# A two-layer transformer trunk on one core: the mirroring of the tokens' mean squares in two steps, and new tables for the order of the work

## The chip, the cores and the metric

The kernel runs on one core of a Trainium2 chip. Its engines each work through a queue of their own, in order: TensorE (PE in the profile; PEld is its loading of weights), VectorE (DVE), ScalarE (ACT), GpSimd (POOL) and SyncE (SP), which here only issues transfers; GpSimd issues some too. The metric is the device time of one execution in microseconds, of which the runs shown give the median.

## The reference

256 tokens of width 2048 pass through two layers, all in float32. What matters here:

```
h = h + attention(rms_norm(h) @ w_in) @ w_out          # layer 1: causal, with forget gates
h = h + relu(rms_norm(h) @ w1)**2 @ w2                 # MLP, inner width 8192
k, v = split(rms_norm(h) @ kv_w)                       # shared keys and values, computed once
q = rms_norm(h) @ w_q
h = h + chunked_attention(q, k, v, rel_bias) @ w_out   # layer 2
h = h + relu(rms_norm(h) @ w1)**2 @ w2
```

Every matrix has 2048 rows (w2 has 8192), so nearly all the work is products of 256 tokens with weights that are read once from memory.

## The kernel before

**Exact products from split weights.** Each weight tile of 128 x 1024 (a *unit*) is taken apart: ScalarE makes a rounded high half (L310, `hi`), VectorE the rest of it (L319, `lo`). TensorE multiplies the activations, split in the same way, three times: high with high (L628), low with high (L630), high with low (L632). So TensorE needs the high half at the start of a unit and the low half at its last third. The function `fetch` hands out the next unit and first writes out as many low and high halves ahead as a table says.

**The pairs.** The two MLPs run in four chunks of the inner width each. One chunk has four *pairs* of column blocks: w10 and w11 (first matrix), w20 and w21 (second matrix). Behind the first MLP stand two further pairs for the query of layer 2, q0 and q1. Within a pair a part of the product is done by seven products in place of eight (Winograd's form of Strassen's method), on weight blocks 11, 12, 21, 22 and their sums. These are the forms f0 to f6, whose weights are 11, T3 = 12 + 22, T2 = T3 + 11, T1 = 11 + 12, 21, T4 = T2 + 21, and 22. A form has two halves of six products each. The rest of a pair are eight *plain* units of twelve products, four called a and four called b. The even pairs (w10, w20, q0) gather in the PSUM tiles `s` and `po`, the odd ones (w11, w21, q1) in `acc`.

The sums of blocks come from several queues. `bring` (L337) has SP fetch block 11 or 12 into a tile of its own, which is free when the pair before is done with it. GpSimd adds blocks from memory onto them for T3 and T1 (L350, a transfer that accumulates). VectorE makes T2 (L357, `make`) and T4 (L348). T4 reads block 21 from the buffer in which it was loaded as a unit; that buffer, one of three of `raw` (loaded at L295 by SP), is free only when both additions for T4 are done.

Between forms, partial sums pass from one PSUM tile to another: behind f0 and f1 by ScalarE (L668, L671), behind f2 by VectorE's subtraction L673, behind f3 by L675. f3 adds onto the tile that L673 reads, so its first product waits for L673.

**The order is written out by tables.**
- `ORDER` gives each pair's forms (f0 to f6), own plain units (a, b) and, as r, plain units that the pair ahead has left over. An r takes nothing where nothing is left. What a pair doesn't name it leaves to the next.
- `LOOK` gives for f0 to f6 and for plain units how many units beyond the present one are made ready before its products are written out; `MORE` allows that many high halves more.
- `BEHIND` hangs `make`, `add` and `bring` behind the low half of a form: (form, half): (how many low halves later, whether for this pair (1) or the next (0), what, ...).
- `HIDDEN`, `LONG`, `SHORT`, `AGAIN`, `QUERY` give, in units (a form counts as one), how long after the end of a column block each step of its further work comes. `HIDDEN` is for the hidden layer's four column blocks: four moves that finish the transposition of a block by transfers (L490; SP and GpSimd issue two each per move), and then relu, square and split (L990 to L1001). `LONG` and `SHORT` are for the stages that make the next layer's input: squares of rows, transpose, four moves, then scaling by the gains (L451), and split (L454, L455). `SHORT` serves the stage ahead of each MLP.
- `OPENING` does for the first pair of an MLP what `BEHIND` does for the others.

These steps are put into the list `fill`; `run_fill` takes one entry after each plain unit and each form.

**The mirroring.** Layer 2's keys and values are computed with the tokens in mirrored order, so the tokens' mean squares (`ms`, 128 x 2) must be mirrored over the partitions as well. `flip` (L611 to L620) does it with a product: VectorE copies the identity matrix with its columns reversed (`flipper`, L614), TensorE multiplies `ms` by it (L615), VectorE copies the result (L618) and scales it (L568), GpSimd takes a power of it (L563). It is one entry of `fill`, `QUERY[6]` = 3 entries behind the end of q0's second column block, which lies in the middle of q1. From there the order of before is f3, b, a, b, with the mirroring behind that b, then f6, a, a, b, b and the first panel of the keys. That panel writes the tiles `acc` that q1 used, so it waits for the norms of the query (L731, `qn`) that still read them.

Of the kernel before, what the change touches and what calls it, by code (L numbers as in the profile page):

```python
# [15 lines left out]
P = 128  # L16
# [27 lines left out]
)  # L44
SHORT = (
# [4 lines left out]
)  # L50
REL = 384
QUERY = (0, 1, 13, 10, 5, 9, 3)
AGAIN = (0, 0, 1, 3, 4, 4, 7, 5)
ATT = ((8, 14, 18, 18, 10), (8, 8, 12, 12, 9), (8, 13, 18, 18, 10), (8, 8, 12, 12, 8))
BIAS = ((3, 6, 7), (3, 6, 4))
LOOK = {
# [6 lines left out]
}  # L63
MORE = {
# [6 lines left out]
}  # L71
ORDER = {
# [9 lines left out]
}  # L82
BEHIND = {
    "w10": {(0, 0): [(0, 1, "make", 0), (7, 1, "add", "T1", 0)], (0, 1): [(2, 1, "add", "T1", 1), (0, 1, "make", 1)], (1, 1): [(1, 0, "bring", "12", 0), (0, 0, "bring", "12", 1)], (3, 1): [(6, 0, "bring", "11", 0), (6, 0, "bring", "11", 1)], (4, 0): [(1, 1, "add", "T4", 0)], (4, 1): [(0, 1, "add", "T4", 1), (9, 0, "add", "T3", 1)], (6, 0): [(0, 0, "add", "T3", 0)]},
    "w11": {(0, 0): [(0, 1, "make", 0), (7, 1, "add", "T1", 0)], (0, 1): [(2, 1, "add", "T1", 1), (0, 1, "make", 1)], (1, 1): [(1, 0, "bring", "12", 0), (1, 0, "bring", "12", 1)], (3, 1): [(5, 0, "bring", "11", 0)], (4, 0): [(0, 1, "add", "T4", 0)], (4, 1): [(0, 1, "add", "T4", 1), (9, 0, "add", "T3", 1)], (6, 0): [(1, 0, "add", "T3", 0)], (2, 1): [(7, 0, "bring", "11", 1)]},
# [30 lines left out]
def trunk(ctx: ExitStack, tc: tile.TileContext, t):  # L116
# [454 lines left out]
    class RowStats:  # L571
# [27 lines left out]
        def spread(self):  # L599
# [9 lines left out]
            yield  # L609

        def flip(self):  # L611
            pm = ps_o.tile([P, 512], F32, name="pt", tag="po")
            flipper = wk.tile([P, P], F32, name="flipper", tag="wk")
            V.tensor_copy(flipper, ident[:, ::-1])  # L614
            TE.matmul(pm[:, :NB], flipper, self.ms, start=True, stop=True)  # L615
# [463 lines left out]
    def query(g):  # L1079
        box = {}  # L1080

        def f(b, ps):
# [124 lines left out]
```

## Time and profile before

| | |
|---|---|
| median of 3 runs | 2105.89 us (2103.67 to 2107.0) |
| the profiled execution's own time | 2103.45 us |
| its span | 2101.7 us, granted clock 0.999 |
| instructions | 26998 |

A row of the timeline has the start in us from the span's beginning, the duration in us, the engine, the line of the code, the operation, what it writes and reads, how many of the same kind follow one another (xN), and in brackets how long the engine idled before it and what ended that. SPq rows are issues of transfers by SP, whose data land later. In a row of waits stand engine, tile and line that waited, then what released it, then the total in us, how many times, and the longest. A row of the chain of waits has start, duration and what the time went to. A row of a stretch has its ends, its length, the busy time and count of PE, PEld, DVE, ACT and POOL, the granted clock, the busy share of the 16 transfer engines and GB/s.

### The profile page before, as it was taken

The numbers are of one execution on the slowest core, as the hardware profiler recorded it, in microseconds if no ns is written. First come the engines' busy times: TensorE is split into PE (matmuls) and PEld (weight loads), VectorE is DVE, ScalarE is ACT, GpSimd is POOL, SyncE is SP. The second block draws the span as 40 slices with busy tenths as digits, with TensorE's granted clock in tenths as the row PEclk, the third lists the DMA queues.
The fourth block names the chain that finished last, engine by engine and source line by source line (L and its number), as shares of the span: only waits on it lengthen the run. The fifth ranks groups of instructions, "written<-read, shape, count | busy, mean of one in ns | idle before, by whom it ended". The sixth has DMA issues, their size and how long they took to land. (4 is left out here: it accounts for less than half of the span.)

```text
span 2101.7 us, 26998 instructions
## 1 busy us (share of the span) xinstructions
PE 2069.0 (98%) x9114; PEld 1696.5 (81%) x9114; DVE 1723.8 (82%) x2003; ACT 1290.3 (61%) x1567; POOL 354.8 (17%) x552
## 2 busy tenths in 40 slices
PE   9999999999999999999999999999999999999999
PEld 7888888787887887887777888887878878878877
DVE  6777676898888889888999576768988998898896
ACT  6544545776667567567777444456765765675674
POOL 1001001231032022022224000022310310220220
PEclk9999999999999999999999999999999999999999
DMA  8777778899898898899886777688997988988884
GB/s 304 242 254 225 238 245 277 259 254 274 258 285 244 250 297 246 264 267 282 251 252 202 260 238 239 226 276 254 265 282 251 271 258 262 286 255 258 267 270 167
DMA packets 160635, 538.89 MB, mean 256 GB/s; under 512 B 42848, under 2 KB 68080, under 8 KB 125680
## 3 DMA queue, kind: packets, MB, share of 16 engines
q1 hardware_dynamic: 129136, 453.78, 60.8%
q0 software_dynamic: 31360, 83.39, 21.4%
q8 instruction: 71, 1.16, 0.2%
q14 instruction: 68, 0.56, 0.1%
HBM read 497.20 MB, written 15.75 MB: 244 GB/s over the span
## 5 line engine op out<-in xcount | busy, mean ns | idle before, releaser
L319 DVE TENSOR_TENSOR lo<-raw,hi 128x1024 fp32r<-128x1024 f32 (+1 forms) x634 | 753.4, 1213 | 149.7 <-ACT hi L310 137.4
L310 ACT ACTIVATE hi<-raw 128x1024 fp32r<-128x1024 f32 (+1 forms) x634 | 651.0, 1052 | 330.0 <-PE acc L630 129.6
L628 PE MATMUL acc<-hi,act 128*128 128x512 f32 x1644 | 456.1, 394 | 5.6 <-ACT hi L310 2.0
L632 PE MATMUL acc<-lo,act 128*128 128x512 f32 x1644 | 449.0, 390 | 1.7 <-DVE lo L319 1.7
L630 PE MATMUL acc<-hi,act 128*128 128x512 f32 x1644 | 448.8, 389 | 0.0
L628 PEld LDWEIGHTS acc<-hi,act 128*128 128x128 f32 x1644 | 306.8, 188 | 71.1 <-ACT hi L310 3.6
L632 PEld LDWEIGHTS acc<-lo,act 128*128 128x128 f32 x1644 | 307.9, 188 | 68.4 <-DVE lo L319 4.3
L630 PEld LDWEIGHTS acc<-hi,act 128*128 128x128 f32 x1644 | 308.5, 188 | 65.2 <-DVE act L421 0.5
L319 DVE TENSOR_TENSOR lo<-w,hi 128x1024 fp32r<-128x1024 f32 x204 | 243.8, 1214 | 18.6 <-ACT hi L310 18.4
L310 ACT ACTIVATE hi<-w 128x1024 fp32r<-128x1024 f32 x204 | 211.3, 1053 | 73.3 <-PE po L630 29.8
L490 POOL DMA_DIRECT2D q<-z x336 | 170.3, 517 | 259.1 <-DVE z L475 95.0
L310 ACT ACTIVATE hi<-wT 128x1024 fp32r<-128x1024 f32 x136 | 140.8, 1054 | 77.4 <-DVE wT L348 48.5
L319 DVE TENSOR_TENSOR lo<-wT,hi 128x1024 fp32r<-128x1024 f32 x136 | 160.3, 1216 | 4.8 <-ACT hi L310 3.7
L628 PE MATMUL s<-hi,act 128*128 128x512 f32 x476 | 136.7, 391 | 4.5 <-ACT hi L310 2.8
L632 PE MATMUL s<-lo,act 128*128 128x512 f32 x476 | 137.0, 392 | 0.6 <-DVE lo L319 0.5
L630 PE MATMUL s<-hi,act 128*128 128x512 f32 x476 | 136.0, 390 | 0.0
L628 PEld LDWEIGHTS s<-hi,act 128*128 128x128 f32 x476 | 89.0, 188 | 25.2 <-ACT hi L310 4.1
L632 PEld LDWEIGHTS s<-lo,act 128*128 128x128 f32 x476 | 88.5, 188 | 22.8 <-DVE lo L319 4.8
L630 PEld LDWEIGHTS s<-hi,act 128*128 128x128 f32 x476 | 88.7, 188 | 19.7 <-DVE act L1001 1.4
L727 POOL TENSOR_TENSOR rn<-vv,mhalf 128x4 f32<-128x4 f32 x32 | 44.4, 1401 | 336.3 <-DVE vv L726 336.2
L350 POOL DMA_DIRECT2D w<-in_f1a x32 | 28.6, 967 | 320.4 <-ACT hi L310 191.2
L357 DVE TENSOR_TENSOR wT<-w,w 128x1024 f32<-128x1024 f32 x68 | 82.7, 1217 | 0.0
(183 smaller groups left out, 2333.4 us busy)
## 6 DMA issues: line engine op xcount, KB each, us to landing
raw<-in_w_in SPq DMA_DIRECT2D x94, 512.0 KB, 5.3
raw<-in_s1a SPq DMA_DIRECT2D x32, 1024.0 KB, 6.8
raw<-in_s2a SPq DMA_DIRECT2D x32, 1024.0 KB, 6.7
raw<-in_w_kv SPq DMA_DIRECT2D x64, 512.0 KB, 5.6
raw<-in_s1b SPq DMA_DIRECT2D x32, 1024.0 KB, 6.7
raw<-in_s2b SPq DMA_DIRECT2D x32, 1024.0 KB, 5.7
raw<-in_w_oa SPq DMA_DIRECT2D x32, 512.0 KB, 5.6
w<-in_f1a SPq DMA_DIRECT2D x16, 1024.0 KB, 6.7
```

What stands on the lines that cost most here:

```text
L310: S.activation(hi[:, c], raw[:, c], AF.Copy)
L319: V.tensor_tensor(lo[:, c], raw[:, c], hi[:, c].bitcast(F32), op=ALU.subtract)
L350: G.dma_start(d, p.big[block][:, half(s)], accum_op=ALU.add)
L357: V.tensor_tensor(p.t["T2"][:, half(s)], p.t["T3"][:, half(s)], p.t["11"][:, half(s)], op=ALU.add)
L490: (SY, G)[j % 2].dma_start(d[32 * j : 32 * j + 32, i], z[32 * i : 32 * i + 32, j * n : (j + 1) * n])
L628: TE.matmul(ps, xh, cut(hi, j), start=first, stop=False, **kw)
L630: TE.matmul(ps, xl, cut(hi, j), start=False, stop=False, **kw)
L632: TE.matmul(ps, xh, cut(lo, j), start=False, stop=last, **kw)
L727: G.tensor_tensor(rn, vv, mhalf, op=ALU.pow)
```

## The change

`flip` gets a second `yield`: the reversed copy is one step, product and all that follows are another, two entries of `fill` later. It begins at `QUERY[6]` = 4 rather than 3. The PSUM tile is taken in the second step.

All the tables are replaced. Taking from `ORDER` what an r really takes, most orders stay as they were. What differs: in w21 one plain unit fewer stands ahead of f6 and one fewer behind f5, so that the next w10 has seven units of its forerunner to place rather than five; in w11 one a moves ahead of f3; in the last chunk's w21 f1 comes ahead of f0; in q1 the tail is f3, b, b, a, a, f6, a, b, b. In w20, T4's first addition comes one low half behind f4's first one rather than two. In w10, w21 and q1 it comes behind the same low half rather than one later. In `HIDDEN` the moves of the second, third and fourth column block come up to two entries sooner.

```diff
 HIDDEN = (
     (3, 3, 3, 5, 8, 9, 9, 10, 11, 12),
-    (0, 2, 3, 3, 5, 7, 7, 7, 9, 9),
-    (1, 1, 3, 3, 5, 5, 8, 9),
-    (1, 3, 4, 4, 7, 8, 9, 9),
+    (1, 2, 2, 2, 5, 7, 7, 7, 9, 9),
+    (0, 1, 1, 2, 5, 5, 7, 9),
+    (0, 1, 4, 4, 7, 8, 9, 9),
 )
 LONG = (
-    (0, 0, 1, 2, 2, 2, 7, 8, 8, 8),
-    (1, 1, 2, 3, 4, 4, 7, 8, 8, 11),
-    (4, 0, 0, 0, 1, 5, 7, 7),
-    (2, 0, 2, 3, 3, 3, 8, 8),
+    (2, 0, 0, 2, 2, 2, 8, 8, 8, 8),
+    (2, 1, 2, 3, 4, 4, 8, 8, 8, 10),
+    (4, 0, 0, 1, 3, 4, 7, 7),
+    (1, 0, 1, 3, 3, 3, 7, 8),
 )
 SHORT = (
-    (7, 0, 0, 0, 1, 1, 4, 5, 6, 6),
-    (9, 0, 1, 1, 5, 7, 8, 12, 13, 14),
-    (1, 0, 1, 1, 2, 4, 5, 8),
-    (8, 0, 1, 2, 2, 3, 4, 4),
+    (8, 0, 0, 0, 0, 1, 4, 4, 8, 8),
+    (7, 0, 1, 1, 5, 7, 8, 12, 13, 14),
+    (2, 0, 1, 4, 4, 4, 6, 8),
+    (7, 0, 1, 2, 2, 3, 5, 5),
 )
-QUERY = (0, 1, 13, 10, 5, 9, 3)
-AGAIN = (0, 0, 1, 3, 4, 4, 7, 5)
+QUERY = (0, 1, 14, 11, 7, 8, 4)
+AGAIN = (0, 0, 2, 2, 4, 4, 6, 5)
-BIAS = ((3, 6, 7), (3, 6, 4))
+BIAS = ((3, 6, 7), (8, 5, 3))
 LOOK = {
-    "w10": (2, 1, 2, 2, 3, 2, 2, 2),
-    "w11": (2, 3, 2, 2, 3, 2, 2, 2),
-    "w20": (2, 1, 2, 2, 1, 2, 2, 2),
-    "w21": (2, 2, 2, 1, 2, 1, 2, 2),
-    "q0": (2, 2, 2, 2, 1, 2, 1, 2),
-    "q1": (2, 2, 2, 2, 3, 2, 2, 2),
+    "w10": (2, 1, 2, 2, 2, 2, 3, 2),
+    "w11": (2, 3, 2, 2, 2, 2, 2, 2),
+    "w20": (2, 1, 2, 2, 1, 1, 3, 2),
+    "w21": (2, 2, 2, 1, 1, 1, 1, 2),
+    "q0": (2, 2, 1, 2, 1, 2, 2, 2),
+    "q1": (2, 3, 2, 2, 2, 2, 2, 2),
 }
...
 ORDER = {
-    "w10": "f0 r r r f1 f2 r f4 f5 f3 a r r a f6 r b a a b",
-    "w11": "f0 f1 r f2 r r r f4 f3 a a a r r f5 a f6 b b",
-    "w20": "r f0 r f1 f2 f4 r f3 f5 a r r a b f6 r",
-    "w21": "f0 f1 f2 r r f3 r f4 r r r r a f6 f5 r a b r",
+    "w10": "f0 r r r f1 f2 r f4 r f5 f3 a r a f6 b r a a b",
+    "w11": "f0 f1 r f2 r r f4 r a f3 a a f5 r a f6 r b b",
+    "w20": "r f0 r f1 f2 f4 r r f3 f5 a r a r r b f6 r",
+    "w21": "f0 f1 f2 r r f3 r f4 r r r r f6 f5 r r a",
...
-    "w21+": "f0 f1 r r f2 r r r r f4 f5 r f3 a r a f6 r a a r r b r b",
+    "w21+": "f1 f0 r r f2 r r r f4 r f5 f3 r r a a r f6 a a r b r r b",
...
-    "q1": "f0 f1 f2 r r a f4 r f5 r f3 b r b r a b f6",
+    "q1": "f0 f1 f2 r r a f4 r f5 r f3 b r b a a f6 r a",
 }
 BEHIND = {
...
-    "w20": {(0, 0): [(7, 1, "add", "T1", 0), (0, 1, "make", 0)], (0, 1): [(0, 1, "make", 1)], (1, 1): [(0, 0, "bring", "12", 0), (1, 0, "bring", "12", 1), (3, 1, "add", "T1", 1)], (3, 1): [(5, 0, "bring", "11", 0), (2, 0, "bring", "11", 1)], (4, 0): [(2, 1, "add", "T4", 0)], (4, 1): [(0, 1, "add", "T4", 1), (8, 0, "add", "T3", 1)], (6, 0): [(0, 0, "add", "T3", 0)]},
+    "w20": {(0, 0): [(7, 1, "add", "T1", 0), (0, 1, "make", 0)], (0, 1): [(0, 1, "make", 1)], (1, 1): [(0, 0, "bring", "12", 0), (3, 1, "add", "T1", 1), (1, 0, "bring", "12", 1)], (3, 1): [(5, 0, "bring", "11", 0), (1, 0, "bring", "11", 1)], (4, 0): [(1, 1, "add", "T4", 0)], (4, 1): [(0, 1, "add", "T4", 1), (7, 0, "add", "T3", 1)], (6, 0): [(0, 0, "add", "T3", 0)]},
...
 }
 OPENING = (
-    (18, "bring", "12", 0),
+    (16, "bring", "12", 0),
     (19, "bring", "12", 1),
-    (9, "add", "T3", 0),
-    (5, "add", "T3", 1),
+    (4, "add", "T3", 0),
+    (6, "add", "T3", 1),
     (4, "bring", "11", 0),
     (14, "bring", "11", 1),
 )
         def flip(self):
-            pm = ps_o.tile([P, 512], F32, name="pt", tag="po")
             flipper = wk.tile([P, P], F32, name="flipper", tag="wk")
             V.tensor_copy(flipper, ident[:, ::-1])
+            yield
+            pm = ps_o.tile([P, 512], F32, name="pt", tag="po")
             TE.matmul(pm[:, :NB], flipper, self.ms, start=True, stop=True)
...
             self.flipped = f
+            yield
...
-                    add_fill([[]] * QUERY[6] + [[st2.flip]])
+                    step = steps(st2.flip)
+                    add_fill([[]] * QUERY[6] + [[step], [], [step]])
```

More of the change, by code (lines that the diff above doesn't have):

```diff
@@ new lines @@
+    "w10": {(0, 0): [(0, 1, "make", 0), (8, 1, "add", "T1", 0)], (0, 1): [(2, 1, "add", "T1", 1), (1, 1, "make", 1)], (1, 1): [(1, 0, "bring", "12", 0), (0, 0, "bring", "12", 1)], (3, 1): [(7, 0, "bring", "11", 0), (4, 0, "bring", "11", 1)], (4, 0): [(0, 1, "add", "T4", 0)], (4, 1): [(0, 1, "add", "T4", 1), (9, 0, "add", "T3", 1)], (6, 0): [(1, 0, "add", "T3", 0)]},
+    "w11": {(0, 0): [(0, 1, "make", 0), (6, 1, "add", "T1", 0)], (0, 1): [(2, 1, "add", "T1", 1), (0, 1, "make", 1)], (1, 1): [(3, 0, "bring", "12", 0)], (3, 1): [(4, 0, "bring", "11", 0)], (4, 0): [(0, 1, "add", "T4", 0)], (4, 1): [(0, 1, "add", "T4", 1), (8, 0, "add", "T3", 1)], (6, 0): [(1, 0, "add", "T3", 0)], (2, 1): [(7, 0, "bring", "11", 1), (2, 0, "bring", "12", 1)]},
@@ new lines @@
+    "w20": {(0, 0): [(7, 1, "add", "T1", 0), (0, 1, "make", 0)], (0, 1): [(0, 1, "make", 1)], (1, 1): [(0, 0, "bring", "12", 0), (3, 1, "add", "T1", 1), (1, 0, "bring", "12", 1)], (3, 1): [(5, 0, "bring", "11", 0), (1, 0, "bring", "11", 1)], (4, 0): [(1, 1, "add", "T4", 0)], (4, 1): [(0, 1, "add", "T4", 1), (7, 0, "add", "T3", 1)], (6, 0): [(0, 0, "add", "T3", 0)]},
+    "w21": {(0, 0): [(0, 1, "make", 0), (7, 1, "add", "T1", 0)], (0, 1): [(0, 1, "make", 1), (0, 1, "add", "T1", 1)], (3, 1): [(5, 0, "bring", "11", 0)], (4, 0): [(0, 1, "add", "T4", 0)], (4, 1): [(0, 1, "add", "T4", 1), (9, 0, "add", "T3", 1), (5, 0, "bring", "11", 1)], (6, 0): [(0, 0, "add", "T3", 0)], (2, 1): [(0, 0, "bring", "12", 0), (1, 0, "bring", "12", 1)]},
```

7 lines of the change are left out of this document (2 added, 5 removed), and 19 rows, old and new, of tables (MORE, ORDER).

## The prediction

> **What bounds the kernel now.** First the busy times of the page, then TensorE's waits, then the chain of waits, then the timeline around one wait of each kind.
>
> ```profile
> PE 2069.0 (98%) x9114; PEld 1696.5 (81%) x9114; DVE 1723.8 (82%) x2003; ACT 1290.3 (61%) x1567; POOL 354.8 (17%) x552
> ...
> PE acc L632 <- DVE lo L319: 8.5, 18, 0.6
> PE po L632 <- DVE lo L319: 4.2, 8, 0.6
> ```
>
> The kernel is bound by TensorE, and its product count doesn't change: all that can be won or lost is waits. The largest group is short and repeated: a low half (L319) that comes late, 18 times at the odd pairs (acc) and 8 times at the even ones (po). A listed wait understates its price:
>
> ```profile
> 833.37 0.62 PE L628 MATMUL acc<-hi,Sh 128*128 128x512 f32 x2
> 833.83 0.63 PE L630 MATMUL acc<-hi,Sh 128*128 128x512 f32 x2
> 835.07 0.73 PE L632 MATMUL acc<-lo,Sh 128*128 128x512 f32 x2 [0.61 <-DVE lo L319]
> ```
>
> Undisturbed, two products follow two others after 0.46 us (833.37 to 833.83). The third group starts 1.24 after the second and lasts 0.11 longer: 1.24 - 0.46 + 0.11 = 0.89 us lost where 0.61 is listed. With 0.28 added for each wait, the 18 cost 8.5 + 18 x 0.28 = 13.5 us and the 8 cost 4.2 + 8 x 0.28 = 6.4 us. The chain of waits says why:
>
> ```profile
> 1859.16 1.15 DVE wT L348
> 1860.37 10.46 DMA raw<-in_f2b
> 1873.16 1.23 DVE lo L319
> ```
>
> An addition for T4, then a load, then low halves. The timeline of one w20 and the w21 behind it (the pattern returns in all eight chunks):
>
> ```profile
> 810.60 1.22 DVE L348 TENSOR_TENSOR wT<-wT,raw 128x1024 f32<-128x1024 f32 x1
> ...
> 811.74 0.68 DVE L673 TENSOR_TENSOR s<-p,po 128x512 f32<-128x512 f32 x1
> ...
> 812.34 1.22 DVE L319 TENSOR_TENSOR lo<-w,hi 128x1024 fp32r<-128x1024 f32 x1
> ...
> 812.91 0.62 PE L628 MATMUL po<-hi,Sh 128*128 128x512 f32 x2
> ...
> 813.47 1.21 DVE L348 TENSOR_TENSOR wT<-wT,raw 128x1024 f32<-128x1024 f32 x1
> ...
> 814.76 0.33 SPq L295 DMA_DIRECT2D raw<-in_f2a  x1
> 815.14 4.42 SPq L490 DMA_DIRECT2D q<-z  x6
> ...
> 815.88 0.73 PE L632 MATMUL po<-lo,Sh 128*128 128x512 f32 x2 [0.52 <-DVE lo L319]
> ...
> 819.73 0.47 SPq L337 DMA_DIRECT2D w<-in_f2a  x1
> ...
> 828.16 2.01 ACT L310 ACTIVATE hi<-w 128x1024 fp32r<-128x1024 f32 x2 [0.31 <-DMA w<-in_f2a]
> ...
> 829.25 1.23 DVE L319 TENSOR_TENSOR lo<-w,hi 128x1024 fp32r<-128x1024 f32 x1 [1.91 <-ACT hi L310]
> ```
>
> The second T4 addition ends at 814.68. Only then is the raw buffer of block 21 free, and the load of block 22 goes out (814.76). Behind it on SP's queue stand six issues of the hidden layer's transposition (4.42 us) and the bringing of block 11 for w21 (819.73), whose data ScalarE gets at 828.16. VectorE has meanwhile idled 1.91 us and then meets, at f0 to f2 of w21, more work than TensorE leaves it time for: the waits at acc. And the transfer engines show a hole at the place of the late load:
>
> ```profile
> 812.00:816.00 4.00, 3.48 (x16) 2.56 (x15) 3.93 (x5) 1.26 (x3) 1.85 (x2) 1.00 0.55 131
> 816.00:820.00 4.00, 4.00 (x18) 3.17 (x18) 4.00 (x5) 3.65 (x4) 0.00 (x0) 1.00 1.02 216
> ```
>
> Busy to 0.55 from 812 to 816, full afterwards.
>
> **The change part by part.**
>
> *T4 in w20 (delay 2 to 1).* Both additions now stand together behind f4's low halves. The second ends at 810.60 + 2 x 1.22 - 0.08 (successive rows overlap by that) = 812.96 instead of 814.68, so the load goes out 1.7 us sooner, into the hole. Two of the six issues behind it stand ahead of it now (last hidden quarter, 1,3 to 0,1), so block 11 could be asked for at 813.0 + 0.3 + 4 x 0.74 = 816.3, 3.4 us sooner. As the transfer engines are full from 816 on, I count 1.7, which is less than VectorE's 1.91 of idle time, so w21's low halves all move up by it. The loss there is 13.5 / 8 = 1.7 us a pair, unevenly spread, and a pair that loses more keeps the rest: I take 1.3 a pair, **-10.5 us**; bounds 0 (the data lands no sooner) and -13.5.
>
> *Its price.* In w20 the first T4 addition now stands ahead of the subtraction L673 (811.74 becomes about 812.96, end 813.64), on whose result f3's first product (812.91) waits; then f3's first low half ends at 814.78 instead of 813.56. Its last products start at 814.85 instead of 813.82, and those of the second half 1.36 later, 816.2 instead of 815.88: **+0.3 a pair, +2.6 us** for eight; bounds 0 and +0.8 a pair (the whole shift of L673).
>
> *The first pair of each MLP (SHORT, last row, steps 4,4 to 5,5).*
>
> ```profile
> 1452.64 1.71 ACT L451 ACTIVATE y<-q,gsb 128x256 f32<-128x256 f32 x4 [2.51 <-DMA q<-z]
> ...
> 1455.34 1.04 ACT L310 ACTIVATE hi<-wT 128x1024 fp32r<-128x1024 f32 x1
> ...
> 1456.43 0.73 PE L628 MATMUL s<-hi,act 128*128 128x512 f32 x2 [1.56 <-ACT hi L310]
> ...
> 1457.88 0.73 PE L632 MATMUL s<-lo,act 128*128 128x512 f32 x2 [0.25 <-DVE lo L319]
> ...
> 408.99 0.74 PE L628 MATMUL s<-hi,act 128*128 128x512 f32 x2 [0.56 <-ACT hi L310]
> ```
>
> ScalarE waits 2.51 us for a transfer, with the high half that f5 needs queued behind it. One form later, that half is ahead of it. Won: 1.84 + 0.53 at 1456, 0.84 at 409, each with its 0.28: **-3.2 us**; bounds 0 and -3.2. What L451 makes is used only by the last plain products; late next would be the high halves behind it, which the units already made cover.
>
> *q0 (look-ahead at f2, 2 to 1).*
>
> ```profile
> 1063.04 2.31 DVE L319 TENSOR_TENSOR lo<-w,hi 128x1024 fp32r<-128x1024 f32 x2
> ...
> 1065.27 0.69 DVE L673 TENSOR_TENSOR s<-p,po 128x512 f32<-128x512 f32 x1
> ...
> 1066.11 0.83 PE L628 MATMUL po<-hi,S 128*128 128x512 f32 x2 [2.93 <-DVE s L673]
> ...
> 1070.51 0.62 PE L628 MATMUL s<-hi,act 128*128 128x512 f32 x2
> ...
> 1072.45 3.49 DVE L319 TENSOR_TENSOR lo<-raw,hi 128x1024 fp32r<-128x1024 f32 x3
> ...
> 1075.06 1.07 PE L632 MATMUL s<-lo,act 128*128 128x512 f32 x4
> ```
>
> One of the two low halves ahead of L673 goes behind it: f3 starts 1.16 sooner. The two halves of f3, twelve products, took 4.40 us (1066.11 to 1070.51) where six times 0.46 make 2.76, so 1.64 more may come back with the clock. But VectorE's work up to the next low half is the same and it has no gap: that half is ready at 1072.45 + 1.22 = 1073.67, and its products can start 1.3 us before 1075.06. **-1.3 us**; bounds 0 and -4.6 (2.93 + 1.64). The Trainium skill (TensorE: Matmul & The Clock Gate, What's actually happening) has the clock halve after an idle window of some 3.4 us; here 2.93 of idle time was enough. By its window the shorter wait is the safer for it, and with the slow stretch kept the gain would be the 1.16 of the earlier start.
>
> *The mirroring.*
>
> ```profile
> 1128.85 0.71 DVE L475 STREAM_TRANSPOSE z<-qn 128x512 f32<-128x512 f32 x1 [1.59 <-DMA land<-z]
> 1129.48 0.18 DVE L614 COPY flipper<-ident 128x128 f32<-128x128 f32 x1
> 1129.81 0.35 PE L615 MATMUL pt<-msb,flipper 128*128 128x2 f32 x2 [0.87 <-DVE flipper L614]
> ...
> 1147.01 0.73 PE L628 MATMUL acc<-hi,act 128*128 128x512 f32 x2 [1.66 <-DVE qn L731]
> ...
> 1119.69:1147.01 27.32, 23.20 (x101) 18.39 (x101) 23.89 (x33) 22.90 (x34) 11.47 (x14) 1.00 0.67 219
> ```
>
> The copy stands behind a transpose that waits for a transfer; TensorE waits 0.87 for it. Copied one fill step later than now and used two further, it is there long before its product: the 0.87 and 0.1 of slowed products go. The second step moves VectorE's copy of the result, its scaling and GpSimd's power by three steps, past GpSimd's issues of the query's transposition; the first K/V panel's norms use them, eight plain units of twelve products (2.76 us each) away. VectorE waits at that copy for TensorE; behind it stand low halves for two units further on. But 17 us later TensorE waits for qn (1147.01), and VectorE is busy 23.89 of these 27.32 us, 1.59 of the rest being that transfer: what is won here is mostly waited for there. **-0.5 us**; bounds 0 and -1.0.
>
> *Order of w21 and w10, the other look-aheads, OPENING, LONG, AGAIN, BIAS.* No wait of the trace is tied to most of them. w21 gives two plain units more to w10, where buffers are full and ScalarE waits for TensorE:
>
> ```profile
> 869.66 1.07 ACT L310 ACTIVATE hi<-raw 128x1024 fp32r<-128x1024 f32 x1 [1.20 <-PE acc L630]
> ```
>
> That cover hides it. I take 0; bounds -1.4 (the rest of the q0 wait) and one late low half a place, 1.22 + 0.28 = 1.5 us (below).
>
> Sum: -10.5 + 2.6 - 3.2 - 1.3 - 0.5 = **-12.9 us**. The profiled execution took 2103.45 (span 2101.7 and 1.75 around it), 2.44 under the median of the runs, 2105.89. Forecast: 2103.45 - 12.9 + 2.44 = **2093.0 us**; its own range, 2088 to 2099.
>
> **The rivals.**
>
> *The load lands no sooner.* The transfer engines are the bound of w20's second half (1.02 of the window). For: they are full right behind the hole; against: the hole itself. The 10.5 stay: -2.4 us, **2103.5**. The Trainium skill (DMA: Bandwidth & Descriptors, Issuing engines are not separate DMA queues) says that transfers of all issuers interleave on the same 16 engines, so an earlier issue only takes turns from others; the 0.55 speaks against it here.
>
> *Less ahead, more late (slower).* The look-ahead at f4 of w10, w11 and w21, f6 of w21 and f5 of w20 is cut by one: 40 places in eight chunks. Where an evacuation holds VectorE until TensorE is done, one prepared unit less leaves a low half late: 1.5 us a place. It evens out the gain at 12.9 / 1.5 = 9 places and is slower from 12. If both of w21's forms do it in all eight chunks: 16 x 1.5 = 24 - 12.9 = +11.1, **2117**. For: VectorE is 82% busy and w21 is where it falls behind; against: the ScalarE wait for TensorE just quoted, behind w21's forms.
>
> *All of it.* w21's 13.5, q0's 4.6, the mirroring's 1.0: -13.5 + 2.6 - 3.2 - 4.6 - 1.0 = -19.7, **2086.2**. Against: VectorE's unbroken work behind q0.
>
> *Mostly dead letters.* Many of the r's added take nothing, as the pair ahead has left nothing; if the delays matter as little, only the mirroring is left: **2105.4**. Against: the chain passes through L348.
>
> **How the numbers follow.** Forecast 0.53, load no sooner 0.17, less ahead 0.17, all of it 0.08, dead letters 0.05. Within 0.2% (4.2 us: 2101.7 to 2110.1) is about what a measurement cannot tell from no change: dead letters and two thirds of the second case, 0.17; slower is the third, 0.17; faster the rest, 0.66. The range reaches from just under the case of all to the edge of no change, 2084 to 2110, leaving out the slower case.
>
> **What would show it.** In w20, the two L348 side by side and the load of block 22 under 0.1 us behind the second; block 11 asked for before 818.5 on this scale; the waits acc <- lo down from 18 to 6 or fewer; po <- lo kept, with waits on L673 (about 0.7 each) new beside it. No wait of over 1 us on ScalarE in the first pairs; q0's wait on L673 at some 1.8 us; no wait on flipper, and that on qn grown. It is wrong if waits of the acc kind stay at about 18 with the load moved up, or if new ones stand at f4 and f6 of w21.

## The result and the profile after

| | before | after |
|---|---|---|
| median of the runs | 2106.43 us (2103.67 to 2107.0, 4 runs) | 2093.23 us (2092.54 to 2093.58, 4 runs) |
| ratio, 95% interval | | 0.994 (0.9922 to 0.9957) |
| profiled execution, its span | 2103.45 us, 2101.7 us | 2092.97 us, 2091.2 us |

The change saves 13.2 us by the medians, 10.5 between the two profiled executions. The forecast was 2093.0. The number fits; several of the terms behind it do not, and the largest is among those.

Behind L620 the lines of the kernel before stand two lower in the changed one (inside `flip` one lower: its L616 is before's L615): its L630, L632 and L634 are the products of before's L628, L630 and L632; L675 is the subtraction that was L673, L733 is the making of `qn` (L731), and L1003 the hidden layer's split (L1001). Of the experiments below, e1 to e3, e6, e8 and e12 have the line numbers of before, the others those of the changed kernel.

Busy times, from the page of the changed kernel:

```profile
PE 2064.7 (99%) x9114; PEld 1697.1 (81%) x9114; DVE 1721.5 (82%) x2003; ACT 1295.5 (62%) x1567; POOL 354.5 (17%) x552
```

The number of products is as before, 9114, and so is VectorE's work. Only waits went. TensorE's waits in the changed kernel (engine, tile and line, what released it, then us in total, times, longest):

```profile
PE po L630 <- DVE s L675: 6.8, 9, 1.8
PE acc L634 <- DVE lo L319: 6.5, 15, 0.6
```

The waits for a low half at `acc`, which were to fall from 18 to 6 or fewer, are still 15. The eight waits of `po` for a low half are gone altogether, and eight waits on L675 of some 0.64 us stand in their place (the ninth is q0's 1.8). There is no wait on `flipper` any more.

The timeline of the changed kernel, with the same w20 and w21 as in the prediction first, then q0, the mirroring, the stage ahead of the second MLP and that MLP's first pair:

```profile
806.80 2.35 DVE L348 TENSOR_TENSOR wT<-wT,raw 128x1024 f32<-128x1024 f32 x2
...
809.22 0.33 SPq L295 DMA_DIRECT2D raw<-in_f2a  x1
809.60 3.26 SPq L490 DMA_DIRECT2D q<-z  x4
...
809.90 0.70 PE L630 MATMUL po<-hi,Sh 128*128 128x512 f32 x2 [0.64 <-DVE s L675]
...
813.02 0.47 SPq L337 DMA_DIRECT2D w<-in_f2a  x1
...
823.44 2.96 ACT L310 ACTIVATE hi<-w 128x1024 fp32r<-128x1024 f32 x3 [1.67 <-DMA w<-in_f2a]
...
1058.92 0.70 PE L630 MATMUL po<-hi,S 128*128 128x512 f32 x2 [1.83 <-DVE s L675]
...
1061.76 0.61 PE L630 MATMUL s<-hi,act 128*128 128x512 f32 x2
...
1066.23 1.19 PE L632 MATMUL s<-hi,act 128*128 128x512 f32 x4 [0.68 <-DVE act L455]
...
1129.43 0.28 PE L616 MATMUL pt<-msb,flipper 128*128 128x2 f32 x2
...
1137.20 0.73 PE L630 MATMUL acc<-hi,act 128*128 128x512 f32 x2 [1.47 <-DVE qn L733]
...
1389.83 1.71 ACT L451 ACTIVATE y<-q,gsb 128x256 f32<-128x256 f32 x4 [8.02 <-DMA q<-z]
...
1393.62 1.21 PE L630 MATMUL acc<-hi,act 128*128 128x512 f32 x4 [1.13 <-ACT hi L310]
...
1443.87 1.69 ACT L451 ACTIVATE y<-q,gsb 128x256 f32<-128x256 f32 x4
```

The first half of the prediction's chain is there to the letter: the two L348 stand side by side (806.80), the load of block 22 goes out 0.07 us behind them (809.22), four issues of the transposition follow in place of six, and block 11 is asked for at 813.02. The second half is not there. ScalarE gets block 11 only at 823.44, having waited 1.67 us for it. The whole place lies 3.80 us sooner in the changed kernel (the first L348 begins at 806.80 in place of 810.60). Beyond that, the load of block 22 was issued 1.7 us sooner (814.76 - 3.80 - 809.22), block 11 was asked for 2.9 sooner (819.73 - 3.80 - 813.02), and it reached ScalarE 0.9 sooner (828.16 - 3.80 - 823.44). From its request to ScalarE it took two microseconds more.

The stretches of the changed kernel around it (from:to, length, busy us of PE, PEld, DVE, ACT, POOL, granted clock, share of the 16 transfer engines, GB/s):

```profile
808.00:812.00 4.00, 3.36 (x15) 2.27 (x14) 4.00 (x6) 3.01 (x4) 1.82 (x2) 1.00 0.83 237
812.00:816.00 4.00, 4.00 (x19) 3.31 (x18) 4.00 (x6) 2.54 (x4) 0.00 (x0) 1.00 1.04 251
816.00:820.00 4.00, 4.00 (x20) 3.30 (x19) 4.00 (x5) 2.02 (x2) 0.00 (x0) 1.00 1.03 203
820.00:824.00 4.00, 4.00 (x19) 3.31 (x18) 1.70 (x2) 1.62 (x2) 0.00 (x0) 1.00 1.02 414
```

The hole of before (0.55) is filled to 0.83, and from 812 on the engines are full: at 251 and 203 GB/s while GpSimd's accumulating transfers run, and at 414 GB/s once they are through. How the two queues share the engines shows it more closely. For 816 to 818 of the changed kernel (queue, packets, MB, share of the 16 engines' time; q0 is here GpSimd's queue and q1 SP's, not the pairs of these names):

```profile
q0 software_dynamic: 86, 0.29, 85.0%
q1 hardware_dynamic: 87, 0.06, 12.0%
```

In steps of 2 us from 814 to 820 GpSimd's queue takes 77, 85 and 92% of the engines' time and SP's, with block 11 in it, 28, 12 and 18%. (In e11 below, without these accumulations, GpSimd's queue moves nothing here from 814 on.) From 822 to 824 SP's has all of it, at 426 GB/s.

**Where the time went.** The table below uses the time lost at a place: over all its products of 512 columns, the distance from one start to the next less the undisturbed 0.227 us, summed. One execution lets a place vary by a microsecond or so, so experiments of the next section that leave a place alone are taken as further executions of it.

| place | predicted | lost with before's tables, us | lost with the changed ones, us | gained |
|---|---|---|---|---|
| the eight w20/w21 chunks | -10.5 + 2.6 | 22.5, 23.4, 25.7, 22.1 | 19.5, 22.2, 20.7 | 2.6 |
| first pairs of the MLPs | -3.2 | 6.4, 5.5, 5.1, 5.7 | 3.6, 1.8, 1.8 | 3.3 |
| q0, around f3 | -1.3 | 6.2, 6.1, 6.2, 6.1, 4.7, 4.7 | 4.7, 4.7, 4.7, 5.0, 5.1, 5.1 | 0.8 |
| mirroring and start of the keys | -0.5 | 5.2, 7.7, 5.2, 5.9 | 3.0, 3.0, 3.1 | 3.0 |
| everything ahead of the first MLP | 0 | 5.6, 5.5, 6.4, 7.0, 6.4 | 5.5, 5.2, 5.7 | 0.7 |

(What is gained is the difference of the means. The first figure of a row is that of before or after itself; the others are those of e1 to e4, and of two of e5, e6 and e9, that leave the place alone. The row of q0 goes from 18 us ahead of f3's first product to 12 us behind it; its figures are those of before, e1, e2, e4, e8 and e12, then of after, e6, e9, e5, e10 and e11.) Together some 10 us of the 13.2; the other 3 are in no place that was looked at.

Three rows are less sure than their means. The two sets of the chunks touch (22.1 and 22.2). The 3.6 of the first pairs holds 1.4 us for a wait that lies ahead of them, at 1393.62, and that the other executions lack; without it the row gains 3.7. In the row of the keys the 7.7, of e1, holds a wait on `flipper` of 1.9 us and a stretch at a lower clock; without e1 that row gains 2.4.

### The profile page after: what moved, and what is told of

The parts are those of the page before. It is cut to its first block, busy times and chain, and to the rows that moved or that the text cites. A ratio compares the mean times of both kernels' runs of the same rounds, so it can differ in the third digit from the quotient of the medians.

```text
span 2091.2 us, 26988 instructions
## 1 busy us (share of the span) xinstructions
PE 2064.7 (99%) x9114; PEld 1697.1 (81%) x9114; DVE 1721.5 (82%) x2003; ACT 1295.5 (62%) x1567; POOL 354.5 (17%) x552
## 4 chain that ended last, share of the span: by engine, by line
PE 81%; DVE 8%; DMA 5%; issue 2%; ACT 2%; SPq 1%; DVEq 0%; POOL 0%; ACTq 0%
PE acc L634 18%; PE acc L630 18%; PE acc L632 18%; DVE lo L319 5%; PE po L630 5%; PE po L632 5%; PE po L634 5%; PE s L632 4%; PE s L634 4%; PE s L630 4%; DMA w<-in_f2a 2%; ACT hi L310 1%; DMA w<-in_f2b 1%; DVE wT L357 1%; PE s L788 1%
## 5 line engine op out<-in xcount | busy, mean ns | idle before, releaser
L630 PE MATMUL acc<-hi,act 128*128 128x512 f32 x1644 | 456.3, 394 | 4.9 <-ACT hi L310 2.3
L634 PE MATMUL acc<-lo,act 128*128 128x512 f32 x1644 | 448.9, 389 | 1.6 <-DVE lo L319 1.6
L632 PE MATMUL acc<-hi,act 128*128 128x512 f32 x1644 | 448.9, 389 | 0.0
L630 PEld LDWEIGHTS acc<-hi,act 128*128 128x128 f32 x1644 | 306.8, 188 | 70.4 <-ACT hi L310 4.3
L634 PEld LDWEIGHTS acc<-lo,act 128*128 128x128 f32 x1644 | 308.1, 188 | 68.0 <-DVE lo L319 3.7
L632 PEld LDWEIGHTS acc<-hi,act 128*128 128x128 f32 x1644 | 308.5, 188 | 65.2 <-DVE act L421 0.5
L310 ACT ACTIVATE hi<-wT 128x1024 fp32r<-128x1024 f32 x136 | 141.4, 1053 | 47.4 <-PE acc L632 22.1
L630 PE MATMUL s<-hi,act 128*128 128x512 f32 x476 | 136.5, 390 | 2.3 <-DVE s L675 1.6
L632 PE MATMUL s<-hi,act 128*128 128x512 f32 x476 | 135.7, 389 | 0.7 <-DVE act L455 0.7
L634 PE MATMUL s<-lo,act 128*128 128x512 f32 x476 | 135.8, 390 | 0.1
L630 PEld LDWEIGHTS s<-hi,act 128*128 128x128 f32 x476 | 89.0, 188 | 22.5 <-DVE s L675 2.4
L632 PEld LDWEIGHTS s<-hi,act 128*128 128x128 f32 x476 | 89.3, 188 | 19.8 <-DVE act L455 1.1
L634 PEld LDWEIGHTS s<-lo,act 128*128 128x128 f32 x476 | 89.2, 188 | 19.3 <-DVE lo L319 0.9
```

Source lines behind the costliest of these rows:

```text
L310: S.activation(hi[:, c], raw[:, c], AF.Copy)
L630: TE.matmul(ps, xh, cut(hi, j), start=first, stop=False, **kw)
L632: TE.matmul(ps, xl, cut(hi, j), start=False, stop=False, **kw)
L634: TE.matmul(ps, xh, cut(lo, j), start=False, stop=last, **kw)
```

## The experiments

Twelve kernels were run, each timed beside the kernel before on the same chip. Medians of the kernel before were 2105.03 us (e1 to e4), 2106.42 (e5, e7, e8, e10), 2106.35 (e6, e9, e11) and 2106.15 (e12).

### One part at a time: e1, e2, e3, e4

Each is the kernel before with one part of the change.

```diff
# e1_t4: BEHIND, w20
-(4, 0): [(2, 1, "add", "T4", 0)]
+(4, 0): [(1, 1, "add", "T4", 0)]
# e2_short: SHORT, last row
-    (8, 0, 1, 2, 2, 3, 4, 4),
+    (8, 0, 1, 2, 2, 3, 5, 5),
# e3_look: LOOK
-    "q0": (2, 2, 2, 2, 1, 2, 1, 2),
+    "q0": (2, 2, 1, 2, 1, 2, 1, 2),
# e4_flip: flip in two steps as in the change, QUERY[6]
-3)
+4)
```

> The kernel before with one number changed: in w20 the first T4 addition comes one low half behind f4's first one, not two. My theory (the late release of block 21's buffer makes w21's low halves late): the load of block 22 goes out 1.7 us sooner in each of the eight chunks, the waits acc <- lo fall from 8.5 us in 18 to under 5 us, and the whole is 4 to 8 us faster in spite of 0.3 us more a pair at f3 (the wait on L673 takes the place of that on lo at po). Rival (the transfer engines are the bound there): block 22 is asked for sooner but block 11 lands less than 0.5 us sooner, the waits acc <- lo stay above 7.5 us, and the whole is within 2 us of before.

Measured: 2103.62 us, ratio 0.9991 (0.9981 to 1.0): 1.4 us, with an interval of 0 to 4. TensorE's waits and the timeline of e1:

```profile
PE po L628 <- DVE s L673: 8.2, 9, 3.0
PE acc L632 <- DVE lo L319: 8.1, 17, 0.6
```

```profile
808.65 2.36 DVE L348 TENSOR_TENSOR wT<-wT,raw 128x1024 f32<-128x1024 f32 x2
...
811.07 0.33 SPq L295 DMA_DIRECT2D raw<-in_f2a  x1
...
815.81 0.46 SPq L337 DMA_DIRECT2D w<-in_f2a  x1
...
826.43 2.01 ACT L310 ACTIVATE hi<-w 128x1024 fp32r<-128x1024 f32 x2 [0.82 <-DMA w<-in_f2a]
```

The whole place lies 1.95 us sooner than in the kernel before (the first L348 at 808.65 in place of 810.60). Beyond that the load goes out 1.7 us sooner and block 11 is asked for 2.0 sooner (819.73 - 1.95 - 815.81), yet it reaches ScalarE no sooner (826.43, where 828.16 - 1.95 is 826.21), and the waits at `acc` hardly change (8.5 in 18 to 8.1 in 17). This is the rival "the load lands no sooner" of the prediction. The price at `po` is there as foreseen: waits on L673 in place of those on the low half.

> The kernel before with SHORT's last row ending in 5, 5 in place of 4, 4. My theory: ScalarE makes f5's high half before it turns to L451, the three waits s <- hi of 2.8 us go, and with the 0.28 that each hides and the late low halves behind them the kernel is 3.2 to 3.7 us faster, nothing else moving. Rival: the next high halves are late instead, and the waits only change their place: within 1 us of before.

Measured: 2102.94 us, ratio 0.9987 (0.9978 to 0.9996): 2.1 us, with an interval of 0.8 to 4.6; the first pairs lose 3.4 us in place of 6.4 (the single profile says 3.0 gained). The term of 3.2 holds, near its size.

> The kernel before with q0's look-ahead at f2 cut from 2 to 1. My theory: f3's wait on L673 falls from 2.9 to about 1.8 us and the granted clock no longer drops behind it (its twelve products take 2.8 us, not 4.4), but VectorE's unbroken work lets only 1.3 us of it come through at the next plain unit, where a new wait stands. Rival: the whole 1.1 + 1.6 = 2.7 us comes through. Other rival: the clock drops all the same, 1.1 us.

Measured: 2105.26 us, ratio 0.9996 (0.9986 to 1.0006), not to be told from no change; the interval goes from 2.9 us faster to 1.3 slower. In the trace the wait of 2.9 us fell to 1.8, q0 loses 4.7 us in place of 6.2, and a wait of 0.3 for VectorE's split L455 stands a little later. A low half of q1 is late by 0.5 us 27 us behind f3. But the 1.5 us at q0 are not the look-ahead's: e8 and e12 lose the same 4.7 with the look-ahead of before. What differs is the clock behind the wait, of which more below (q0).

> The kernel before with the mirroring in two steps, begun at entry 4, and no other table changed. My theory: the wait on flipper (0.9 us) goes, and the wait on qn at the first panel of the keys (1.7 us) grows by nearly as much, since VectorE has little idle time between: 0 to 0.6 us faster in all. Rival: the 1.0 us comes through.

Measured: 2102.81 us, ratio 0.999 (0.9981 to 1.0): 2.2 us. The wait on `flipper` is gone, and from the waits of e4:

```profile
PE acc L630 <- DVE qn L733: 2.9, 2, 1.7
```

Before it was 1.7 in one and 0.75 on ScalarE's squares. So about half of the 0.9 us that was won stands at `qn` again: the place loses 4.6 in place of 5.2. The timing's 2.2 is more than that; its interval, 0 to 4 us, holds both.

### The four together: e7

> The kernel before with the four parts that were tried one by one, together: T4 in w20, the last row of SHORT, the look-ahead of q0, the mirroring in two steps. Theory (the parts add): 1.4 + 2.1 + 0.4 + 2.2 = 6 us under the kernel before by their timings, 7 to 8 by their places in the traces, so 2097 to 2099, and the other 5 to 6 us of the changed kernel come from tables not yet tried. Rival (the parts depend on one another, a wait that was won by one being handed on until the next is gone as well): 10 us or more under the kernel before, within 3 us of the changed kernel.

Measured: 2098.59 us, ratio 0.9962 (0.995 to 0.9974): 7.8 us. The parts add within the noise: 1.4 + 2.1 + 2.2 by the medians of three, and nothing that can be told for e3, 5.7 in all, each with an interval of some 2 us either way. The remaining 5.4 us of the changed kernel come from tables not among them.

### The pair tables, without and with two numbers of SHORT: e8, e12

e8 is the kernel before with the rows `first`, w10, w11, w20, w21, w20+ and w21+ of ORDER, LOOK, MORE and BEHIND as changed. e12 is e8 and

```diff
 SHORT = (
-    (8, 0, 1, 2, 2, 3, 4, 4),
+    (8, 0, 1, 2, 2, 3, 5, 5),
```

> The kernel before with the order, the look-ahead and the places behind the low halves of the changed kernel for the pairs of the MLPs (first, w10, w11, w20, w21), and nothing else of the change: T4's earlier place is in it, the new rows of HIDDEN, LONG and SHORT, q0, q1 and the mirroring are not. Theory (the rest of the gain in w21 comes from the pair tables: two plain units more left to w10, look-ahead cut): waits acc <- lo at 6 to 7 us in all, 4 to 5 us faster than the kernel before. Rival (the moves of the hidden layer and of the next input, HIDDEN and LONG, did it): like T4's place alone, 1 to 2 us faster, acc <- lo at 8 or more.

Measured: 2106.89 us, ratio 1.0 (0.9989 to 1.0011). Neither theory: the waits at `acc` fell as the first one said, and the time did not. Waits, timeline and one stretch of e8:

```profile
PE s L632 <- DVE lo L319: 6.2, 2, 3.8
PE acc L632 <- DVE lo L319: 5.1, 13, 0.6
```

```profile
1452.48 1.71 ACT L451 ACTIVATE y<-q,gsb 128x256 f32<-128x256 f32 x4 [2.80 <-DMA q<-z]
...
1455.31 1.23 DVE L455 TENSOR_TENSOR act<-y,act 128x1024 fp32r<-128x1024 f32 x1 [4.90 <-ACT act L454]
...
1457.73 1.22 PE L632 MATMUL s<-lo,act 128*128 128x512 f32 x2 [3.76 <-DVE lo L319]
```

```profile
1457.70:1464.00 6.30, 6.27 (x15) 4.99 (x16) 5.65 (x5) 3.65 (x7) 0.00 (x0) 0.51 0.14 29
```

The eight chunks lost 18.9 us in place of 22.5 (about 21 in e12, which has the same tables there). But at the first pair of either MLP ScalarE waits for the transfer at L451, VectorE waits 4.90 us for ScalarE at L455, and the low half that TensorE needs next is queued behind both: waits of 2.46 and 3.76 us, and behind the second the granted clock is 0.51 over 6.3 us. The first pairs lost 12.1 us.

> The kernel before with the pair tables of the changed kernel (as in the run of these alone) and, beside them, only the two numbers of SHORT's last row, 5, 5 in place of 4, 4. Theory (the pair tables do save the 3.6 us that their run showed in the eight chunks, and lost them at the two first pairs, where L451, L454 and L455 stand ahead of a high and a low half that the new order no longer has in store): the two waits s <- lo of up to 3.8 us at the first pairs go, the places of the first pairs lose 3 us in place of 12.1, so 8 to 9 us faster than the pair tables alone, 2097 to 2099. Rival (those halves are late because of the order of the first pair or of OPENING's transfers, whatever stands in SHORT): at least one wait s <- lo of over 2 us stays, 2102 or more.

Measured: 2095.59 us, ratio 0.9948 (0.9935 to 0.9962), 11.3 us under e8. The first pairs lose 1.8 us. So two numbers that save 2.1 us on the kernel before save 11.3 on the pair tables: these leave less in store at the first pair, and SHORT's later place takes away what would be waited for. Four fifths of the whole gain (10.6 of 13.2) are in e12; q0, the mirroring and q1 add the rest.

### T4's place inside the change: e5

```diff
 "w20": ...
-(4, 0): [(1, 1, "add", "T4", 0)]
+(4, 0): [(2, 1, "add", "T4", 0)]
```

> The changed kernel with one number put back: in w20 the first addition for T4 comes two low halves behind f4's again. Theory (what one part alone showed: the transfer engines, not the time of the request, set when block 11 lands, so T4's earlier place is worth 1 to 3 us): 1 to 3 us slower than the changed kernel, about 2094.5 to 2096.5, the eight waits po <- s of some 0.65 replaced by eight waits po <- lo of 0.5, acc <- lo at 6.5 to 8.5 us in all. Rival, the prediction's term: 7.9 us slower (10.5 less 2.6), about 2101, acc <- lo near 8.5 in 18. Second rival: what w21 gained comes from the other tables alone, within 0.7 us of the changed kernel.

Measured: 2096.74 us (2092.79 to 2098.34), ratio to before 0.9948 (0.9935 to 0.9961); slower than the changed kernel by 3.5 us by the medians and by 1.7 by the two ratios (0.9948 against 0.994), whose intervals overlap. Waits and timeline of e5:

```profile
PE acc L634 <- DVE lo L319: 7.6, 16, 0.6
PE po L634 <- DVE lo L319: 3.8, 8, 0.6
```

```profile
818.15 0.46 SPq L337 DMA_DIRECT2D w<-in_f2a  x1
...
827.75 2.96 ACT L310 ACTIVATE hi<-w 128x1024 fp32r<-128x1024 f32 x3 [0.56 <-DMA w<-in_f2a]
```

This place lies 3.40 us later than in the changed kernel (its first L348 begins at 810.20). Beyond that block 11 is asked for 1.7 us later (818.15 - 3.40 - 813.02) and reaches ScalarE 0.9 later (827.75 - 3.40 - 823.44). That is the theory's mechanism, and the time lies in its range or a little over it, well under the 7.9 of the prediction. Whether the earlier place is worth more inside the change than alone (e1, 1.4 us) can't be told, and the time by itself does not exclude the second rival.

### The mirroring inside the change: e6

The changed kernel with `flip` in one step, `QUERY[6]` = 3.

> The changed kernel with the mirroring in one step again, at entry 3, all tables as changed. Theory (the first step hides the copy, the tables of q1 and of the second making of the input did the rest of the 2.2 us at this place): a wait on flipper of 0.9 to 1.9 us comes back, the wait on qn stays at 1.5 or falls to 0.5 at the least, 0.3 to 1.2 us slower than the changed kernel. Rival (the two steps are what won the place): the place loses 5.2 us again in place of 2.96, 2 us slower or more.

Measured: 2093.88 us, 0.65 over the changed kernel, with ranges that overlap (2093.27 to 2095.14). Waits of e6:

```profile
PE acc L628 <- DVE qn L731: 0.8, 1, 0.8
...
PE pt L615 <- DVE flipper L614: 0.4, 1, 0.4
```

0.4 us on `flipper` comes back and the wait on `qn` shrinks from 1.5 to 0.8: the place loses 2.9 us with one step and 3.0 with two. The theory holds at its lower end; inside the change the two steps by themselves are worth no more than the noise. What won the place is the rest: with the two steps and the old tables it still loses 4.6 (e4) or 5.2 (e7).

### What holds block 11: e10, e11

e10 is the changed kernel with the fourth column block's last two moves, and the relu after them, one place later. On SP's queue the request for block 11 then comes ahead of the moves' four issues.

```diff
 HIDDEN = (
-    (0, 1, 4, 4, 7, 8, 9, 9),
+    (0, 1, 5, 5, 8, 8, 9, 9),
```

> The changed kernel with the last two moves of the hidden layer's fourth column block one place later (4, 4 to 5, 5 in the last row of HIDDEN) and the relu behind them too (7 to 8): in w20 the request for block 11 then stands ahead of the moves' four issues on SP's queue rather than behind them, and is held only by its buffer, free at 812.0 of the changed kernel's timeline in place of 813.02. Theory (block 11 is late because its packets queue behind the moves' small ones, which take turns with GpSimd's accumulations from 814 to 820): block 11 reaches ScalarE 2 us sooner or more, the waits acc <- lo of w21 fall from 6.5 to below 4 us, 3 to 7 us faster than the changed kernel. Rival (the engines' whole load in these us is the bound): the accumulations for T3 or the moves land later by what block 11 wins, acc <- lo stays at 6 to 7, the time within 1.5 us of the changed kernel or slower by the wait for the moves.

Measured: 2103.47 us (2099.85 to 2108.01), ratio 0.9986 (0.9976 to 0.9995): 10 us slower than the changed kernel, more than either theory had. Its timeline, a w21 of the second chunk, then the w20 shown above (2.97 us later in this execution), then a w21 of the second MLP:

```profile
668.99 1.22 DVE L1003 TENSOR_TENSOR act<-q,act 128x1024 fp32r<-128x1024 f32 x1 [1.18 <-ACT q L999]
670.13 2.35 DVE L319 TENSOR_TENSOR lo<-wT,hi 128x1024 fp32r<-128x1024 f32 x2
...
671.41 0.73 PE L634 MATMUL acc<-lo,Sh 128*128 128x512 f32 x2 [1.87 <-DVE lo L319]
...
815.01 0.33 SPq L337 DMA_DIRECT2D w<-in_f2a  x1
...
825.67 2.01 ACT L310 ACTIVATE hi<-w 128x1024 fp32r<-128x1024 f32 x2 [2.98 <-DMA w<-in_f2a]
...
1546.66 1.05 PE L634 MATMUL acc<-lo,Sh 128*128 128x512 f32 x2 [1.87 <-DVE lo L319]
```

and its stretches, the one of the late request first:

```profile
815.00:819.00 4.00, 4.00 (x19) 3.32 (x18) 4.00 (x5) 2.40 (x3) 0.00 (x0) 1.00 1.03 292
...
671.40:675.40 4.00, 3.99 (x18) 3.30 (x19) 4.00 (x5) 2.81 (x4) 0.90 (x2) 1.00 0.41 170
...
1546.60:1550.60 4.00, 3.94 (x10) 3.11 (x11) 3.70 (x5) 2.94 (x3) 1.69 (x2) 0.57 0.26 74
```

Block 11 is asked for 0.98 us sooner (815.01 less 2.97 against 813.02) and arrives 0.74 sooner (825.67 less 2.97 against 823.44), not 2: the moves' small packets were not what held it. The engines are full (1.03) with the accumulations either way. And the moved relu, square and split of the hidden layer now fall where w21 makes f2's weights: L1003 waits for ScalarE with f2's low halves behind it, and TensorE waits 1.9 us in six of the eight chunks (11.9 us in all are listed for low halves at `acc`, 6.5 in the changed kernel). That is the larger part of the price (the eight chunks lose between 7 and 8 us more than in the changed kernel and its like); it is not one of the transfers.

e11 leaves the accumulations for T3 of w21 out:

```diff
-        else:
+        elif (name, p.key) != ("T3", "w21"):
             G.dma_start(d, p.big[block][:, half(s)], accum_op=ALU.add)
```

> The changed kernel without the two accumulating transfers that GpSimd issues for T3 of each w21 (16 of 0.5 MB in all; the sum T3 = 12 + 22 is left out there, so f1 multiplies block 12 alone). Theory (the accumulations hold the 16 transfer engines for the 6 to 7 us in which block 11 is asked for, and block 11 in turn holds ScalarE and VectorE): block 11 lands within 4 us of its request at about 813, ScalarE's wait of 1.67 us for it is gone, the waits acc <- lo fall from 6.5 us to below 2, the lost time at the w20/w21 places (19.5 us in eight chunks) falls by 8 to 11, so 2082 to 2086. Rival (VectorE's own work at the start of w21 makes its low halves late, whatever lands when): acc <- lo stays at 5 us or more, the time within 2 us of the changed kernel, 2091 to 2095.

Measured: 2087.91 us (2086.76 to 2089.76), 5.3 under the changed kernel: between the two theories. ScalarE's wait for block 11 was to go and is still 1.50. Waits, timeline and one stretch of e11:

```profile
PE acc L634 <- DVE lo L319: 3.1, 8, 0.4
```

```profile
809.94 5.24 SPq L490 DMA_DIRECT2D q<-z  x4
...
815.34 0.46 SPq L337 DMA_DIRECT2D w<-in_f2a  x1
...
821.88 1.06 ACT L310 ACTIVATE hi<-w 128x1024 fp32r<-128x1024 f32 x1 [1.50 <-DMA w<-in_f2a]
```

```profile
812.00:816.00 4.00, 4.00 (x20) 3.29 (x19) 4.00 (x5) 2.78 (x3) 0.00 (x0) 1.00 0.68 229
```

The waits at `acc` are halved in number and in time, so about half of what is still waited for there hangs on the accumulations; by the lost time the eight chunks are some 3 us better, of the 5.3. They do not hold all of it. With the engines at 0.68 the four issues of moves take SP 5.24 us in place of 3.26, block 11 is asked for at 815.34, and it lands some 6.5 us after its request, sooner than the 10.4 of the changed kernel but not within the 4 that the theory had. Why the moves take SP longer there, and why a megabyte takes that long on engines that are partly idle, was not tried.

### A last attempt at more: e9

In the changed kernel's timeline above ScalarE waits 8.02 us at L451 (1389.83) in the stage ahead of the second MLP, and TensorE 1.13 us behind it (1393.62). e9 gives SHORT's first row what the change gave its last:

```diff
-    (8, 0, 0, 0, 0, 1, 4, 4, 8, 8),
+    (8, 0, 0, 0, 0, 1, 5, 5, 8, 8),
```

> The changed kernel with the scaling by the gains one place later in the first row of SHORT (4, 4 to 5, 5), as the change itself does in the last row: ScalarE then meets L451 behind one more high half rather than waiting 8 us for its transfer with the halves queued behind it. Theory: the wait of 1.1 us for a high half in the stage ahead of the second MLP (at 1393.62 in the changed kernel) goes, 0.5 to 1.5 us faster than the changed kernel, 2092. Rival (the wait is handed on to the split behind it, or was the chance of one execution): within 0.5 us of the changed kernel.

Measured: 2092.84 us (2091.86 to 2095.04) against 2093.23: no difference that can be told. The wait is not there in e9, but neither is it in e5 and e6, which have the changed kernel's own row: the chance of one execution, as the rival said. No version that does the whole work is measurably faster than the changed kernel.

## Why the prediction was right, and where not

**w20 and w21, predicted -10.5 + 2.6, measured -2.6.** The step that failed: "As the transfer engines are full from 816 on, I count 1.7", taken as the time by which block 11 would *land* sooner, and then "w21's low halves all move up by it". The load's request moved by the 1.7 us and block 11's by 2.9 of the 3.4 that were said; the landing moved by 0.9 us. The hole of before was used, 0.83 of it in place of 0.55, but behind it the engines are full without a break to 824, and from 814 to 820 most of their time goes to GpSimd's accumulations. The rival "the load lands no sooner" had this mechanism, with a chance of 0.17. It is shown by e1 (block 11 asked for 2.0 us sooner and landing no sooner, 1.4 us in all), by e5 (a request 1.7 us later that lands 0.9 later) and, from the other side, by e11: with the 8 MB of accumulations left out, 5.3 us more are gained, and the waits at `acc` are halved. The sign that the prediction named for being wrong, waits at `acc` of about 18 with the load moved up, all but came: they are 15. The sentence of the Trainium skill that was set against the hole (DMA: Bandwidth & Descriptors, Issuing engines are not separate DMA queues: transfers of all issuers interleave on the same 16 engines) was the better guide; this trace agrees with it by the 2.9 us of earlier request that became 0.9 of earlier landing.

The price at `po` had the right place and release (L675 for the low half). By the lost time of these eight places it is 7.8 us after against 6.6 before: 1.2 us, half of what was set, inside its bounds.

**First pairs, predicted -3.2, measured -3.3 to -3.7.** Right in place and size, and by the mechanism named: no ScalarE wait at L451 holds a high half, and L451 (1443.87) begins with no idle time ahead of it. What the prediction missed is how much hangs on it. Something like the rival "less ahead, more late" is real, and e8 shows where: with the pair tables, the shorter look-ahead among them, the first pairs lose 12.1 us, unless SHORT takes the transfer's wait off ScalarE. It is not quite that rival, which had VectorE held by an evacuation; here ScalarE's wait at L451 holds it. Which of the pair tables empties the store was not tried apart. The prediction summed the terms one by one and gave this coupling no row.

**q0, predicted -1.3, measured -0.8, and not by the whole mechanism.** The wait is 1.83 as said ("at some 1.8 us"), and a new one of 0.68 stands 7 us later. The slow stretch behind the old wait is gone from this execution: f3's twelve products take 2.84 us (1058.92 to 1061.76) in place of 4.40. But the shorter wait is not what removed it. e12 has the q0 of before, e5 that of the changed kernel; f3's first products and the first behind its twelve:

```profile
1064.07 0.70 PE L628 MATMUL po<-hi,S 128*128 128x512 f32 x2 [2.99 <-DVE s L673]
...
1066.91 0.62 PE L628 MATMUL s<-hi,act 128*128 128x512 f32 x2
```

```profile
1063.90 0.95 PE L630 MATMUL po<-hi,S 128*128 128x512 f32 x2 [1.86 <-DVE s L675]
...
1068.31 0.62 PE L630 MATMUL s<-hi,act 128*128 128x512 f32 x2
```

The twelve take 2.84 us behind the long wait of e12 and 4.41 behind the short one of e5. With the q0 of before, four executions of six are slow there (before, e1, e2, e4, but not e8 and e12); with that of the changed kernel, three of six (e5, e10, e11). At full clock q0 loses 4.7 us with either, so there the shorter look-ahead wins nothing: VectorE's unbroken work sets when the next product can start, as foreseen. Where the clock drops, q0 loses 6.1 to 6.2 us with the tables of before and 5.0 to 5.1 with the changed ones, 1.1 less. That before was slow there in the execution that was predicted from, and the changed kernel not in its own, is luck; why the clock drops in one execution and not in the next stays open.

**The mirroring, predicted -0.5, measured -0.6 in e4 and nothing that can be told in e6.** The wait on `flipper` went. In e4 about half of it was waited for at `qn`; in the changed kernel that wait did not grow, as the prediction's sign had it, but is 1.47 in place of 1.66. The place gains 2.4 to 3.0 us, and most of that was among the edits costed at nothing. The likeliest are q1's new tail and the new places of AGAIN and QUERY, since e12, with the pair tables but the old ones of these, still loses some 5 us. The first panel of the keys now waits once for `qn` (1.47), where it waited 0.75 for ScalarE's squares and then 1.66 for `qn`. Which of those tables does it was not tried apart; "no wait of the trace is tied to most of them" was wrong for these, since the quoted wait on `qn` was tied to them.

**The sum.** -12.9 was predicted, 13.2 saved. That the two agree is in part luck: w20 and w21, the largest term, gave 5 us less than was counted, edits that were costed at nothing gave some 3 more, and another 3 lie in no place that was looked at. Of the 2.44 us added for the distance of the profiled execution to the median, 1.6 can be seen in the table: by so much the means for before's tables lie above that execution's own figures (0.9 in the chunks, -0.7 at the first pairs, 0.8 at the start of the keys, 0.6 ahead of the first MLP).

## What to carry to other kernels

A transfer that is asked for sooner lands sooner only by what the engines had free in between: read the share *and* the GB/s of the stretch from request to landing, and price the move by the free part, not by the time of the request. When tables shift work, look for the place with the least in store (here the first pair of a stage): there new tables and a blocking wait act on each other, and edits that are worth 2 and 0 alone are worth 11 together. Before a slow stretch of the clock, or its absence, is put down to an edit, look for it in other executions with the same tables. A wait that is named in the profile should have each edited table checked against it before any table is costed at nothing.

## What the runs showed of the hardware

- GpSimd's accumulating transfers fill the 16 engines at a third of the rate of plain loads: 141 GB/s at a share of 0.97 from 816 to 818 in the kernel before, where SP's queue moves no packet, and 426 GB/s at 1.01 from 822 to 824 in the changed kernel, where only SP's queue runs.
- One and the same wait can cost the clock or not. In e10 a wait of 1.87 us at 671.41 left the granted clock at 1.00 for the next 4 us; a wait of 1.87 at 1546.66 in the same execution was followed by 0.57, ten products in 4 us in place of 18. At q0 a wait of 2.93 to 2.99 us was followed by slow products in four executions of six, one of 1.83 to 1.87 in three of six. So the length of one wait alone does not decide. The Trainium skill (TensorE: Matmul & The Clock Gate, What's actually happening) has a free-running window, which fits that; its idle window of some 3.4 us is longer than any of these waits, and there the runs decide.
- The kernel before varies from run to run: 2102.2 to 2111.5 us in 71 executions, at mean granted clocks of 0.998 in 37 of them and 0.999 in 31. The slow stretch at q0, worth up to 1.5 us, comes and goes between executions and is one source; what the others are was not settled. The changed kernel's four executions lie within 1.1 us, which is too few to say that it varies less.
